# A hybrid attention layer on one core: all K steps of the up blocks at one alignment in SBUF

## The chip, the cores and the metric

The kernel runs on one core of a Trainium2 chip. A core has TensorE (PE: matmuls, and PEld for its weight loads), VectorE (DVE), ScalarE (ACT), GpSimd (POOL) and SyncE (SP, which here issues DMAs). The metric is the device time of one execution in microseconds; the kernel before takes 1034.46 us (median of three runs, 1034.37 to 1036.26).

## The reference

One decoder layer over 16 meta tokens and 256 tokens of width 2048. Only the last part matters for the change, after attention, pooling and the first layer norm:

```python
mix = jnp.concatenate([attn_out, pool_out], axis=-1) @ w_o[l]
h = layer_norm(ALPHA * h + mix, ln1_g[l], ln1_b[l])
# conv_gated_ffn:
z = h @ w_up                                   # 2048 -> 2 x 5632
z = sum(zp[:, j:j + T] * conv_w[j] for j in range(3)) + conv_b
a, g = jnp.split(z, 2, axis=-1)
f = (jax.nn.gelu(a) * g) @ w_down
h = layer_norm(ALPHA * h + f, ln2_g[l], ln2_b[l])
```

All inputs are float32.

## The kernel before

**Precision in two parts.** Every operand of a large product is split into an upper part (rounded to the type that TensorE reads in one pass) and a lower part (the remainder). A product is then three matmuls: upper times upper, lower weights times upper activations, upper weights times lower activations.

**Weight tiles.** The weights come as a stream of tiles of 128 x 2048 float32 (1 MB each): query and value projections, pool columns, 16 blocks of `w_o` (the *output blocks*), then 88 blocks of `w_up` mixed with blocks of `w_down`. SyncE fetches each into `wraw` (three buffers). `split_part` (L166) writes the upper part with ScalarE (L170) and the lower with VectorE (L171) into `whl` (three buffers of 4224 elements), in two halves of 1024 columns. Tiles are asked for two ahead (`weights`, L237).

**A block.** An output or up block is 128 output channels. `product` (L268) goes through its 16 K steps of 128 inputs each. A K step is three matmuls with the weights `whl` stationary and the activations moving, 258 columns wide: first L275 (upper, upper), then twice L278 (for these blocks, which are "turned": lower weights with upper activations, then upper weights with lower activations). Each matmul loads its own 128 x 128 weights, which PEld does while the matmul ahead of it runs. The permutations `K_O` and `K_UP` set in which order the K steps come.

**Places.** Where in `whl` the two parts lie is a setting of the kind of block, in elements: `OUTPUT = (0, 2048, True)` puts the upper part at 0 and the lower at 2048. `UP = (12, 12 + 2112, True, 512, 52)` puts the upper at 12 and the lower at 2124, and has a *lead*: columns from 512 on, that is K steps 4 to 15, lie 52 elements further, at 64 and 2176 plus their column. In bytes modulo 256, the first four K steps (the lead) lie at 12 x 4 = 48, and the other twelve at 64 x 4 = 256, so 0, as the output blocks do. The half of a tile that holds the boundary at 512 is written as two runs of 512 elements with the gap between them (the class `Split` and the helper `like` see to that); the other half is one run of 1024.

**The feed-forward stage.** `plan` puts up blocks and down tiles in turn. The first eight up blocks are *folded* (L956): they run on `fold`, 260 columns wide, before the layer norm's statistics are known. The other 80 run on the normalised `hp`, 258 columns. From the tenth of these on, up to the last, a down tile (`seven`, L862: 9 or 12 matmuls of 512 columns at L873 to L875, `whl` moving this time) follows nearly every up block. Convolution, gate and the sums of the Winograd-like down product follow on ScalarE, VectorE and GpSimd.

Of the kernel before, what the change touches and what calls it, by code (L numbers as in the profile page):

```python
# [98 lines left out]
QUERY = (10, 10 + 2048, False)  # L99
HEAD = (12, 12 + 2048, True)  # L100
OUTPUT = (0, 2048, True)
UP = (12, 12 + 2112, True, 512, 52)
DOWN = (56, 56 + 2048)


def places(n, kind):

    if kind:
        return UP if kind == "up" else DOWN
    return (QUERY, HEAD, OUTPUT)[(n >= 8) + (n >= 26)]  # L110
# [1062 lines left out]
```

## Time and profile before

| | |
|---|---|
| median of three runs | 1034.46 us |
| profiled execution | 1035.45 us, of it the span 1033.7 |
| TensorE busy | 1025.6 us |
| VectorE busy | 890.8 us |
| ScalarE busy | 621.1 us |
| GpSimd busy | 185.4 us |
| mean granted clock of TensorE | 0.998 |
| output blocks | from about 208 to 299 us |
| folded blocks | from about 300 to 347 us |
| up blocks on `hp` | from 347.5 us on, with down tiles from about 400 us on |

A row of the timeline has the start in us, the time in us, the engine, line, operation, what it writes and reads, and how many such instructions were merged. A matmul's own time (278 to 290 ns) is longer than the distance to the next one (115 to 127 ns), since matmuls are pipelined: what a matmul costs is the distance from its start to the next start. A row of the stretch table has the stretch, its length, then busy time and instructions of PE, PEld, DVE, ACT and POOL, the granted clock, the DMA share and GB/s. A row about one line of the kernel has the shortest, median and longest duration in ns and the first and last start.

### The profile page before, as it was taken

To read this page: it belongs to the slowest core of one execution; us is meant where nothing else is said; L and a number is where in the kernel's file an instruction comes from. 1 tells how busy PE (TensorE), PEld (TensorE's weight loads), DVE (VectorE), ACT (ScalarE), POOL (GpSimd) and SP (SyncE) were. 2 spreads that over 40 slices of the span, in tenths; PEclk is the share of its full clock that TensorE was granted. 3 is DMA by queue.
4 is the path that set the end of the run, shared out by engine and by line. 5 is a ranking of instruction groups with operands and counts; after the bars stand their busy time and mean duration, and the time that the engine had idled before them with its cause. 6 is when DMAs were issued, how large, how long until landed. Compare 5 with 4: busy or idle time off the path is not lost.

```text
span 1033.7 us, 19199 instructions
## 1 busy us (share of the span) xinstructions
PE 1025.6 (99%) x7644; PEld 976.8 (94%) x7644; DVE 890.8 (86%) x1401; ACT 621.1 (60%) x1000; POOL 185.4 (18%) x245
## 2 busy tenths in 40 slices
PE   9999999999999999999999999999999999999997
PEld 8999999999999999999999999999999999999986
DVE  6878668758879998998999999989999999999876
ACT  6656346645549855565666556565556565566675
POOL 1200014125430021120121101211112111120031
PEclk9999999999999999999999999999999999999999
DMA  9655643454554578978887788887978779887874
GB/s 328 243 187 210 226 154 106 145 194 168 200 196 137 194 225 242 287 281 288 291 277 266 277 296 275 269 277 266 300 264 286 270 278 288 277 276 274 289 235 142
DMA packets 59754, 250.28 MB, mean 242 GB/s; under 512 B 21734, under 2 KB 22416, under 8 KB 32656
## 3 DMA queue, kind: packets, MB, share of 16 engines
q1 hardware_dynamic: 34592, 230.42, 62.1%
q0 software_dynamic: 7888, 16.14, 8.2%
q10 hardware_dynamic: 17184, 2.49, 1.5%
q8 instruction: 60, 0.98, 0.4%
q14 instruction: 30, 0.25, 0.1%
HBM read 232.50 MB, written 2.11 MB: 227 GB/s over the span
## 4 chain that ended last, share of the span: by engine, by line
PE 94%; issue 2%; DVE 1%; DMA 1%; POOL 1%; ACT 0%; POOLq 0%; SPq 0%; DVEq 0%; ACTq 0%
PE mm L278 47%; PE mm L275 24%; PE at L873 6%; PE at L875 6%; PE at L874 6%; PE mm L349 2%; DMA wraw<-in_w_down 1%; DVE whl L171 1%; PE mm L577 0%; PE at L438 0%; PE at L612 0%; PE at L439 0%; POOL gb L992 0%; DMA wraw<-in_w_first 0%; PE at L324 0%
## 5 line engine op out<-in xcount | busy, mean ns | idle before, releaser
L171 DVE TENSOR_TENSOR whl<-wraw,whl 128x1024 fp32r<-128x1024 f32 (+1 forms) x416 | 486.5, 1204 | 37.0 <-ACT whl L170 36.0
L170 ACT ACTIVATE whl<-wraw 128x1024 fp32r<-128x1024 f32 (+1 forms) x416 | 402.7, 1015 | 99.3 <-DVE wraw L182 20.6
L278 PE MATMUL mm<-hp,whl 128*128 128x258 f32 x2560 | 459.6, 281 | 0.0
L278 PEld LDWEIGHTS mm<-hp,whl 128*128 128x128 f32 x2560 | 395.5, 189 | 3.1
L275 PE MATMUL mm<-hp,whl 128*128 128x258 f32 x1280 | 362.2, 283 | 0.0
L275 PEld LDWEIGHTS mm<-hp,whl 128*128 128x128 f32 x1280 | 240.4, 188 | 3.2
L278 PE MATMUL mm<-xp,whl 128*128 128x256 f32 (+5 forms) x768 | 140.2, 282 | 0.0
L278 PEld LDWEIGHTS mm<-xp,whl 128*128 128x128 f32 x768 | 118.7, 189 | 0.5
L275 PE MATMUL mm<-xp,whl 128*128 128x256 f32 (+5 forms) x384 | 112.0, 292 | 0.0
L808 ACT ACTIVATE z<-mm,cv 128x256 f32<-128x256 f32 x40 | 22.6, 564 | 97.7 <-PE mm L278 97.7
L845 POOL TENSOR_TENSOR forms<-za 128x128 f32<-128x128 f32 x20 | 21.2, 1062 | 307.1 <-DVE za L826 240.5
L275 PEld LDWEIGHTS mm<-xp,whl 128*128 128x128 f32 x384 | 72.2, 188 | 1.0 <-issue 0.5
L875 PE MATMUL at<-whl,gp 128*128 128x512 f32 x180 | 70.7, 394 | 0.0
L874 PE MATMUL at<-whl,gp 128*128 128x512 f32 x180 | 70.7, 394 | 0.0
L873 PE MATMUL at<-whl,gp 128*128 128x512 f32 x180 | 69.4, 395 | 0.0
L808 ACT ACTIVATE za<-mm,cv 128x256 f32<-128x256 f32 x40 | 22.6, 564 | 75.6 <-PE mm L278 67.9
L848 POOL TENSOR_TENSOR forms<-za 128x128 f32<-128x128 f32 x20 | 20.3, 1014 | 199.8 <-DVE za L826 199.8
L278 PE MATMUL mm<-fold,whl 128*128 128x260 f32 x256 | 46.3, 283 | 0.0
L278 PE MATMUL mm<-mixp,whl 128*128 128x258 f32 x256 | 45.4, 278 | 0.0
L278 PE MATMUL mm<-mixa,whl 128*128 128x258 f32 x256 | 45.2, 278 | 0.0
L875 PEld LDWEIGHTS at<-whl,gp 128*128 128x128 f32 x180 | 33.8, 188 | 8.1
L874 PEld LDWEIGHTS at<-whl,gp 128*128 128x128 f32 x180 | 33.9, 188 | 6.8
(339 smaller groups left out, 1607.8 us busy)
## 6 DMA issues: line engine op xcount, KB each, us to landing
wraw<-in_w_up SPq DMA_DIRECT2D x88, 1024.0 KB, 5.0
wraw<-in_w_down SPq DMA_DIRECT2D x80, 1024.0 KB, 6.3
wraw<-in_w_proj SPq DMA_DIRECT2D x24, 1024.0 KB, 5.4
wraw<-in_w_o SPq DMA_DIRECT2D x16, 1024.0 KB, 4.9
y<-v POOLq DMA_DIRECT2D x27, 256.0 KB, 8.5
y<-u POOLq DMA_DIRECT2D x18, 256.0 KB, 4.9
wraw<-in_w_first SPq DMA_DIRECT2D x8, 304.0 KB, 5.4
x<-in_xt SPq DMA_DIRECT2D x1, 2176.0 KB, 8.0
```

The source lines that it names most:

```text
L170: upper = nc.scalar.activation(hl[:, 0, c], like(raw[:, c], hl, c), AF.Copy)
L171: lower = nc.vector.tensor_tensor(hl[:, 1, c], like(raw[:, c], hl, c), hl[:, 0, c].bitcast(F32), op=ALU.subtract)
L275: nc.tensor.matmul(ps, wh, ah, start=n == 0, stop=False)
L278: nc.tensor.matmul(ps, a, b, start=False, stop=i == 1 and n == KT - 1)
L349: nc.tensor.matmul(ps[:m, :T], hl[:, t // 2, a0 + a:a0 + a + m], x_parts[k][:, t % 2, :], start=k == 0 and t == 0, stop=k == KT - 1 and t ...
L808: nc.scalar.activation(z, src[:, 2:NQ], AF.Identity, bias=col(C_B, j), scale=col(C_W, 3 * j + 2))
L845: nc.gpsimd.tensor_tensor(s[:, 0], a21, a22, op=ALU.add)
L848: nc.gpsimd.tensor_tensor(s[:, 3], a11, a21, op=ALU.subtract)
L873: nc.tensor.matmul(ps, a[:, 0, i], hl[:, 0, w], start=j == 0, stop=False)
L874: nc.tensor.matmul(ps, a[:, 0, i], hl[:, 1, w], start=False, stop=False)
L875: nc.tensor.matmul(ps, a[:, 1, i], hl[:, 0, w], start=False, stop=j == n - 1)
```

## The change

The places of the up and folded blocks become those of the output blocks, without a lead:

```diff
 QUERY = (10, 10 + 2048, False)
 HEAD = (12, 12 + 2048, True)
 OUTPUT = (0, 2048, True)
-UP = (12, 12 + 2112, True, 512, 52)
+UP = (0, 2048, True)
 DOWN = (56, 56 + 2048)
```

All sixteen K steps of these 88 blocks then lie at 0 modulo 256 bytes from the start of `whl`, upper and lower; for K steps 4 to 15 that residue is what it was. TensorE's instructions and their order stay the same; only the addresses of the weights differ. On ScalarE and VectorE the half with the boundary becomes one run of 1024. On VectorE among the last output blocks, where the first folded tiles are split (the second row is the first half of such a tile):

```order
 L732 TENSOR_TENSOR x<-x,acc 128x258
-L171 TENSOR_TENSOR whl<-wraw,whl 128x2x512
+L171 TENSOR_TENSOR whl<-wraw,whl 128x1024
 L746 SCALAR_TENSOR_TENSOR fold<-x,cv,fold 128x258
 L171 TENSOR_TENSOR whl<-wraw,whl 128x1024
 L715 SCALAR_TENSOR_TENSOR x<-x,mm 128x258
```

Nothing moved: the shape of the write is all that differs.

## The prediction

> **What bounds the kernel now.** The page comes first, then the stretch table of the feed-forward stage, then TensorE's timeline row by row at the starts of K steps.
>
> ```profile
> span 1033.7 us, 19199 instructions
> PE 1025.6 (99%) x7644; PEld 976.8 (94%) x7644; DVE 890.8 (86%) x1401; ACT 621.1 (60%) x1000; POOL 185.4 (18%) x245
> ...
> PE 94%; issue 2%; DVE 1%; DMA 1%; POOL 1%; ACT 0%; POOLq 0%; SPq 0%; DVEq 0%; ACTq 0%
> ...
> L278 PE MATMUL mm<-hp,whl 128*128 128x258 f32 x2560 | 459.6, 281 | 0.0
> ...
> L275 PE MATMUL mm<-hp,whl 128*128 128x258 f32 x1280 | 362.2, 283 | 0.0
> ```
>
> The chain that ended last is TensorE's for 94% of the span. The two groups are the up blocks on `hp`: 1280 K steps of three matmuls, so 80 blocks of 16 steps. Their busy times overlap (matmuls are pipelined), so I read the cost of a step from start to start. The stretch of the feed-forward stage shows that nothing else holds them up:
>
> ```profile
> 434.00:970.00 536.00, 536.00 (x3854) 505.32 (x3853) 494.41 (x680) 319.16 (x445) 84.52 (x100) 1.00 0.83 279
> ```
>
> TensorE is busy for all 536.00 us at a granted clock of 1.00; VectorE for 494.41 us (92%). The edit must therefore act through the spacing of matmuls that never wait for another engine. That spacing isn't one number. First an output block of 16 steps (its first, its last, and the next block's first row), then two up blocks in a row, with the down matmuls between them:
>
> ```profile
> 266.24 0.28 PE L275 MATMUL mm<-mixp,whl 128*128 128x258 f32 x1
> 271.44 0.28 PE L275 MATMUL mm<-mixp,whl 128*128 128x258 f32 x1
> 271.78 0.28 PE L275 MATMUL mm<-mixp,whl 128*128 128x258 f32 x1
> ...
> 442.51 0.28 PE L275 MATMUL mm<-hp,whl 128*128 128x258 f32 x1
> 443.95 0.28 PE L275 MATMUL mm<-hp,whl 128*128 128x258 f32 x1
> 444.30 0.28 PE L275 MATMUL mm<-hp,whl 128*128 128x258 f32 x1
> 448.11 0.39 PE L873 MATMUL at<-whl,right 128*128 128x512 f32 x1
> ...
> 450.20 0.28 PE L275 MATMUL mm<-hp,whl 128*128 128x258 f32 x1
> 451.63 0.28 PE L275 MATMUL mm<-hp,whl 128*128 128x258 f32 x1
> 451.98 0.29 PE L275 MATMUL mm<-hp,whl 128*128 128x258 f32 x1
> 456.02 0.40 PE L873 MATMUL at<-whl,right 128*128 128x512 f32 x1
> 458.12 0.28 PE L275 MATMUL mm<-hp,whl 128*128 128x258 f32 x1
> ```
>
> The output block takes 271.78 - 266.24 = 5.54 us, 0.346 a step. The first up block spends 1.44 us on its four lead steps (0.36 each) and then (448.11 - 444.30)/11 = 0.346 on each of its last eleven. The second spends 1.43 us on its lead (0.358) and (456.02 - 451.98)/11 = 0.367 on each of the last eleven. So the rest of a block, whose places are already those of the output blocks modulo 256 bytes, runs in one of two steady patterns, **fast** (0.346) and **slow** (0.367), and keeps it to its end. Blocks take 5.60 and 5.82 us in turn; far later it is the same:
>
> ```profile
> 948.61 0.28 PE L275 MATMUL mm<-hp,whl 128*128 128x258 f32 x1
> 954.21 0.39 PE L873 MATMUL at<-whl,right 128*128 128x512 f32 x1
> 956.30 0.28 PE L275 MATMUL mm<-hp,whl 128*128 128x258 f32 x1
> 962.12 0.40 PE L873 MATMUL at<-whl,right 128*128 128x512 f32 x1
> ```
>
> Again 5.60 and 5.82. In the nine blocks ahead of the first down matmuls the order is slow, fast, and a third, **middle** pattern:
>
> ```profile
> 347.54 0.28 PE L275 MATMUL mm<-hp,whl 128*128 128x258 f32 x1
> 353.36 0.29 PE L275 MATMUL mm<-hp,whl 128*128 128x258 f32 x1
> 358.95 0.28 PE L275 MATMUL mm<-hp,whl 128*128 128x258 f32 x1
> 360.72 0.28 PE L275 MATMUL mm<-hp,whl 128*128 128x258 f32 x1
> 364.61 0.29 PE L275 MATMUL mm<-hp,whl 128*128 128x258 f32 x1
> ```
>
> 5.82, 5.59, then 5.66 with (364.61 - 360.72)/11 = 0.354 a step. Equal places, three spacings: the pattern is chosen by the state in which the block is entered, and the lead sits exactly where that choice is made.
>
> **The change part by part.** *Splits.* The first half of each up and folded block is written by ScalarE and VectorE in one run of 1024 elements in place of two of 512. While the folded blocks run, both kinds of halves fall into these two rows:
>
> ```profile
> L171 DVE TENSOR_TENSOR whl<-wraw,whl x14: 1212/1218/1226, 300.9 to 342.6; 128x1024 fp32r<-128x1024 f32 x14
> L170 ACT ACTIVATE whl<-wraw x15: 1036/1048/1062, 299.8 to 343.4; 128x1024 fp32r<-128x1024 f32 x15
> ```
>
> Shortest to longest differ by 14 and 26 ns. The gap costs at most that, over 88 halves 1.2 us on VectorE and 2.3 on ScalarE, under the 8% that VectorE is idle and far more on ScalarE. On the path: nothing; uncovered, at most those sums. If TensorE gains 12 us of some 570, VectorE's share goes from 92 to 94%, still under TensorE's. No DMA, wait or instruction moves.
>
> *Folded blocks*, 260 columns wide:
>
> ```profile
> 318.68 0.28 PE L275 MATMUL mm<-fold,whl 128*128 128x260 f32 x1
> 320.12 0.28 PE L275 MATMUL mm<-fold,whl 128*128 128x260 f32 x1
> 324.45 0.28 PE L275 MATMUL mm<-fold,whl 128*128 128x260 f32 x1
> ```
>
> Lead 1.44/4 = 0.360, the rest 4.33/12 = 0.361: no pattern is held and the lead costs what the rest costs. I take zero; bounds from the fast and slow steps above, 8 x 16 x (0.346 - 0.361) = -1.9 us and +0.8.
>
> *Up blocks.* Sixteen equal steps in a held pattern take 16 x 0.346 = 5.54 us (fast; the output block is the row for it), 16 x 0.354 = 5.66 (middle), 16 x 0.367 = 5.87 (slow). Today a pair takes 5.60 + 5.82 = 11.42. After the nine early blocks 71 remain, 35.5 pairs. All fast: 11.08 a pair, -0.34 x 35.5 = -12.1; the early three cost 364.61 - 347.54 = 17.07 and would cost 16.62, three times -0.45 = -1.4. Together -13.5. All slow: +0.32 x 35.5 + 3 x 0.54 = +13.0. These are the bounds of the one unknown, the pattern.
>
> Which value? The places that the change gives were entered from outside four times in the output stage, the nearest rows:
>
> ```profile
> 208.78 0.28 PE L275 MATMUL mm<-mixp,whl 128*128 128x258 f32 x1
> 209.12 0.28 PE L275 MATMUL mm<-mixp,whl 128*128 128x258 f32 x1
> ...
> 211.67 0.28 PE L275 MATMUL mm<-mixa,whl 128*128 128x258 f32 x1
> 212.73 0.28 PE L275 MATMUL mm<-mixa,whl 128*128 128x258 f32 x1
> ...
> 217.60 0.28 PE L275 MATMUL mm<-mixp,whl 128*128 128x258 f32 x1
> 220.38 0.28 PE L275 MATMUL mm<-mixa,whl 128*128 128x258 f32 x1
> ...
> 239.19 0.28 PE L275 MATMUL mm<-mixp,whl 128*128 128x258 f32 x1
> 240.24 0.28 PE L275 MATMUL mm<-mixp,whl 128*128 128x258 f32 x1
> ```
>
> Steps of 0.34 after the pool blocks, 1.06/3 = 0.353 after the value products, 2.78/8 = 0.348 after the pooled maps, 1.05/3 = 0.35 (0.346 within the rows' rounding) after the mean: three fast, one middle, none slow. And fast held on: the block from 266.24 us, quoted above, comes several blocks after the last of these entries. I take fast for most blocks, with an estimated entry cost of 0.015 us a block (the steps around 239 us are 0.004 over 0.346, taken for four steps: 71 x 0.015 = +1.1) and, also an estimate, one block in six in the middle pattern as the four entries leave room for it (12 x 0.12 = +1.4). Sum: -13.5 + 1.1 + 1.4 = -11.0. The profiled execution took 1035.45 us (1033.7 of span, 1.75 around it), 1.0 over the median of 1034.46; so 1024.4 against the profile, 1023.5 against the median, which is what I predict.
>
> The row that bears on a rule: equal steps of three 128x258 matmuls take 0.346 or 0.367 us. The Trainium skill ("TensorE: Matmul & The Clock Gate", Step-by-step: what each phase is for) says that TensorE reads its moving operand and its weights through two independent ports, so that loading the next weights takes nothing from the running matmul. By that, places could change nothing and the time would stay at 1034.5. The trace shows that equal instructions at full clock do differ by 6%, though not that the ports are why.
>
> **The rivals.**
> *Slow lock.* The run of down matmuls hands every block a state that leads to the slow pattern, and no lead is left to shift it. For it: 35 of 71 blocks now run slow with these very places after step 4, and the state after a slow block recurs. Against: no slow step in the output stage. Price +13.0 in full, 1047.5; it decides from the point where more than half of the blocks are slow (three in four: about +6, 1040.5).
> *Middle pattern for all.* 5.66 a block: -0.10 x 35.5 - 3 x 0.09 = -3.8, so 1030.7. Seen in one of four entries and one of three early blocks.
> *Nothing changes.* Fast and slow blocks still alternate, because the down matmuls flip the state from block to block: 5.54 + 5.87 = 11.41 against 11.42, the lead was worth nothing, 1034.5. The alternation over 560 us speaks for it; that the lead starts alike in both kinds (1.44 and 1.43) and yet parts them speaks against.
>
> **How the numbers follow.** Mostly fast 0.41, middle 0.12, nothing 0.13, slow lock 0.34, in part or in full. Below 1021.5 is less than all fast without any entry cost; above 1043 lies the full slow lock, about 0.17. So the range is 1021.5 to 1043; the likeliest case's own is 1021.5 to 1029. Faster by over 0.2% (what a measurement of this kernel can tell): 0.41 + 0.12 = 0.53; within 0.2%: 0.13; slower: 0.34.
>
> **What would show it.** In TensorE's timeline the first rows (L275) of steps 0 to 15 of every up block stand 0.346 us apart, in the blocks of both turns, and blocks are 5.54 to 5.57 long; folded blocks keep 0.36; the split rows keep 1218 and 1048 ns; VectorE's share rises. Wrong would be steps of 0.367 from the first on, or blocks that still come in two lengths.

## The result, and the profile after

The changed kernel takes 1025.62 us in the median of five runs (1024.8 to 1029.97), the kernel before 1034.48 us beside it: a ratio of 0.9919, 95% interval 0.9896 to 0.9943. The forecast was 1023.5 us, in a range of 1021.5 to 1043. The profiled execution after took 1025.62 us, 9.83 less than that of before (1035.45).

The page of the changed kernel, its lines for the span, the engines, the chain that ended last, the two split groups and the two groups of the up blocks:

```profile
span 1023.8 us, 19199 instructions
...
PE 1016.8 (99%) x7644; PEld 966.6 (94%) x7644; DVE 889.9 (87%) x1401; ACT 622.1 (61%) x1000; POOL 186.7 (18%) x245
...
PE 94%; issue 2%; DMA 1%; DVE 1%; POOL 1%; ACT 0%; SPq 0%; POOLq 0%; DVEq 0%; ACTq 0%
...
L171 DVE TENSOR_TENSOR whl<-wraw,whl 128x1024 fp32r<-128x1024 f32 (+1 forms) x416 | 486.2, 1203 | 43.7 <-ACT whl L170 42.7
L170 ACT ACTIVATE whl<-wraw 128x1024 fp32r<-128x1024 f32 (+1 forms) x416 | 402.5, 1014 | 114.6 <-DMA wraw<-in_w_up 27.9
L278 PE MATMUL mm<-hp,whl 128*128 128x258 f32 x2560 | 450.3, 279 | 0.0
...
L275 PE MATMUL mm<-hp,whl 128*128 128x258 f32 x1280 | 357.6, 279 | 0.0
```

The limit is where it was: TensorE is still 99% busy and 94% of the chain. The up blocks' busy time fell from 459.6 to 450.3 us on L278 and from 362.2 to 357.6 on L275. The stretch of the feed-forward stage (its length; busy us of TensorE, its weight loads, VectorE, ScalarE and GpSimd; then granted clock, DMA share, GB/s):

```profile
434.00:970.00 536.00, 536.00 (x3913) 504.35 (x3912) 499.64 (x687) 325.27 (x452) 85.02 (x100) 1.00 0.85 284
```

TensorE is full here as before, at the same granted clock of 1.00, but does 3913 matmuls in these 536 us where it did 3854. VectorE went from 494.41 to 499.64 us. The time thus came from the spacing of the same matmuls. TensorE's timeline shows it: the first row of block 52 (counted from the query blocks; the first up block on `hp`), then the first row of blocks 54, 61, 66, 68 and 130 with the row behind the block. L275 opens a K step, L873 opens the down matmuls behind the block.

```profile
346.68 0.28 PE L275 MATMUL mm<-hp,whl 128*128 128x258 f32 x1
...
358.02 0.28 PE L275 MATMUL mm<-hp,whl 128*128 128x258 f32 x1
...
363.57 0.28 PE L275 MATMUL mm<-hp,whl 128*128 128x258 f32 x1
...
399.64 0.28 PE L275 MATMUL mm<-hp,whl 128*128 128x258 f32 x1
...
405.51 0.40 PE L873 MATMUL at<-whl,gp 128*128 128x512 f32 x1
...
441.50 0.28 PE L275 MATMUL mm<-hp,whl 128*128 128x258 f32 x1
...
447.36 0.40 PE L873 MATMUL at<-whl,right 128*128 128x512 f32 x1
...
457.12 0.28 PE L275 MATMUL mm<-hp,whl 128*128 128x258 f32 x1
...
462.70 0.40 PE L873 MATMUL at<-whl,gp 128*128 128x512 f32 x1
...
954.86 0.28 PE L275 MATMUL mm<-hp,whl 128*128 128x258 f32 x1
...
960.42 0.39 PE L873 MATMUL at<-whl,right 128*128 128x512 f32 x1
```

Block 54 takes 5.55 us (16 steps of 0.3467), blocks 61 and 66 take 5.87 and 5.86 (the slow pattern), block 68 5.58 and block 130 5.56. Read from the starts of all 1280 steps, blocks 61 to 66 are slow (5.85 on average) and all 65 blocks from 67 to 131 are fast, at 5.569 us each: their first three steps take 0.360, 0.352 and 0.348 us, the others 0.347. Before, 35 of the 71 blocks from 61 on were slow. The 80 up blocks together went from 456.32 to 447.29 us, 9.03 less. A further 0.86 us lies ahead of them (block 52 began at 347.54 us before, and now at 346.68), where the change does almost nothing. It is not the change's work: block 28, ahead of everything that was changed, already began 1.30 us earlier (at 206.43 in place of 207.73), and the 14 profiles of this case have it anywhere from 206.1 to 207.7 us. Together that is the 9.9 us between the two spans.

### The profile page after: what moved, and what is told of

The parts are those of the page before. It is cut to its first block, busy times and chain, and to the rows that moved or that the text cites. A ratio compares the mean times of both kernels' runs of the same rounds, so it can differ in the third digit from the quotient of the medians.

```text
span 1023.8 us, 19199 instructions
## 1 busy us (share of the span) xinstructions
PE 1016.8 (99%) x7644; PEld 966.6 (94%) x7644; DVE 889.9 (87%) x1401; ACT 622.1 (61%) x1000; POOL 186.7 (18%) x245
## 4 chain that ended last, share of the span: by engine, by line
PE 94%; issue 2%; DMA 1%; DVE 1%; POOL 1%; ACT 0%; SPq 0%; POOLq 0%; DVEq 0%; ACTq 0%
PE mm L278 47%; PE mm L275 24%; PE at L875 6%; PE at L873 6%; PE at L874 6%; PE mm L349 1%; DMA wraw<-in_w_down 1%; DVE whl L171 1%; DMA wraw<-in_w_first 1%; POOL gb L992 0%; PE mm L577 0%; PE at L438 0%; PE at L612 0%; PE at L439 0%; PE at L324 0%
## 5 line engine op out<-in xcount | busy, mean ns | idle before, releaser
L171 DVE TENSOR_TENSOR whl<-wraw,whl 128x1024 fp32r<-128x1024 f32 (+1 forms) x416 | 486.2, 1203 | 43.7 <-ACT whl L170 42.7
L170 ACT ACTIVATE whl<-wraw 128x1024 fp32r<-128x1024 f32 (+1 forms) x416 | 402.5, 1014 | 114.6 <-DMA wraw<-in_w_up 27.9
L278 PE MATMUL mm<-hp,whl 128*128 128x258 f32 x2560 | 450.3, 279 | 0.0
L278 PEld LDWEIGHTS mm<-hp,whl 128*128 128x128 f32 x2560 | 390.6, 188 | 3.4
L275 PE MATMUL mm<-hp,whl 128*128 128x258 f32 x1280 | 357.6, 279 | 0.0
L275 PEld LDWEIGHTS mm<-hp,whl 128*128 128x128 f32 x1280 | 240.4, 188 | 3.1
L278 PE MATMUL mm<-xp,whl 128*128 128x256 f32 (+5 forms) x768 | 140.2, 282 | 0.0
L278 PEld LDWEIGHTS mm<-xp,whl 128*128 128x128 f32 x768 | 118.7, 189 | 0.5
L275 PE MATMUL mm<-xp,whl 128*128 128x256 f32 (+5 forms) x384 | 112.0, 292 | 0.0
L275 PEld LDWEIGHTS mm<-xp,whl 128*128 128x128 f32 x384 | 72.3, 188 | 1.0 <-issue 0.5
L875 PE MATMUL at<-whl,gp 128*128 128x512 f32 x180 | 71.2, 396 | 0.0
L874 PE MATMUL at<-whl,gp 128*128 128x512 f32 x180 | 70.6, 393 | 0.0
L873 PE MATMUL at<-whl,gp 128*128 128x512 f32 x180 | 69.5, 396 | 0.0
L278 PE MATMUL mm<-fold,whl 128*128 128x260 f32 x256 | 46.3, 283 | 0.0
L278 PE MATMUL mm<-mixp,whl 128*128 128x258 f32 x256 | 45.6, 279 | 0.0
L278 PE MATMUL mm<-mixa,whl 128*128 128x258 f32 x256 | 45.4, 279 | 0.0
L875 PEld LDWEIGHTS at<-whl,gp 128*128 128x128 f32 x180 | 33.8, 188 | 8.2
L874 PEld LDWEIGHTS at<-whl,gp 128*128 128x128 f32 x180 | 33.8, 188 | 6.8
```

The lines of the kernel that those rows point to most:

```text
L170: upper = nc.scalar.activation(hl[:, 0, c], like(raw[:, c], hl, c), AF.Copy)
L171: lower = nc.vector.tensor_tensor(hl[:, 1, c], like(raw[:, c], hl, c), hl[:, 0, c].bitcast(F32), op=ALU.subtract)
L275: nc.tensor.matmul(ps, wh, ah, start=n == 0, stop=False)
L278: nc.tensor.matmul(ps, a, b, start=False, stop=i == 1 and n == KT - 1)
L873: nc.tensor.matmul(ps, a[:, 0, i], hl[:, 0, w], start=j == 0, stop=False)
L874: nc.tensor.matmul(ps, a[:, 0, i], hl[:, 1, w], start=False, stop=False)
```

## The experiments

All are edits of the changed kernel. Times are compared with the kernel before on the same chip, since its own median differed between chips (1034.5 to 1038.8); block lengths and totals of the 80 up blocks come from the profiles, where the changed kernel has 447.3 us and the kernel before 456.3.

**Is it the equality modulo 256 bytes, or the form?** First the two runs that keep the equality and change something else.

```diff
-UP = (0, 2048, True)
+UP = (0, 2112, True, 512, 64)      # lead and gap kept, the gap 256 bytes
```

> The lead and its gap are kept, but the gap is 64 elements (256 bytes), so all sixteen places are equal modulo 256 bytes and each first half is still written in two runs of 512. Theory of equal places modulo 256 bytes: as the changed kernel, 1025 to 1030, up blocks of 5.57 us. Rival, that the split's form (two runs of 512) cost the time: up blocks of 5.60 and 5.82 us in turn, 1034.5.

Measured 1026.98 us, ratio 0.9924 (0.9909 to 0.9940). The up blocks take 447.3 us in all, as with the change. Block 69:

```profile
464.78 0.28 PE L275 MATMUL mm<-hp,whl 128*128 128x258 f32 x1
...
470.36 0.40 PE L873 MATMUL at<-whl,gp 128*128 128x512 f32 x1
```

5.58 us, the first six blocks behind a down run slow again and the others fast. The split in two runs of 512 costs the path nothing; the places alone make the gain.

```diff
-UP = (0, 2048, True)
+UP = (64, 64 + 2112, True)         # where steps 4 to 15 lay before
```

> The up and folded blocks lie at offset 64 and 64 + 2112 of their tile, which is where steps 4 to 15 lay before the change; there is no lead. Modulo 256 bytes this equals the changed kernel. Theory of the held pattern (equal places modulo 256 bytes hand the pattern on): about the changed kernel's time, 1024.5 to 1030, with equal steps of 0.347 us in most up blocks. Rival, that the lower offsets or the shorter distance between the two halves (2048 in place of 2112 elements) made the gain: 1031 to 1047, with steps of 0.367 us in half of the blocks or more.

Measured 1026.17 us, ratio 0.9921 (0.9890 to 0.9952), 448.1 us of up blocks. From block 61 on every block has the length it has with the change; blocks 53 to 60 ran in the middle pattern (5.65 us) in this execution. Moving all places by 256 bytes changes nothing from there on, as the forecast assumed when it counted places modulo 256 bytes.

**Was the mixture bad, or the lead's places?**

```diff
-UP = (0, 2048, True)
+UP = (12, 12 + 2112, True)         # all sixteen steps at the old lead's places
```

> All sixteen steps of the up and folded blocks lie at the old lead's offset, 12 elements, with the old distance of 2112 between the halves. Theory that only equality counts (any equal place holds some pattern, and mostly the fast one): 1024 to 1030, steps of 0.347 us. Theory that the place counts too, because the weights then stand 32 bytes from the moving operand's places in place of 8: steps of about 0.354 to 0.361 us, as in the old lead and in the folded blocks, and 1280 x (0.354 to 0.361 - 0.349) = 6 to 15 us more than the changed kernel, 1032 to 1041. Rival that the lead's places were bad in themselves and the mixture did nothing: 0.367 us in every step, 1047.

Measured 1036.10 us, ratio 1.0003 (0.9986 to 1.0019). Blocks 69 and 73:

```profile
466.35 0.28 PE L275 MATMUL mm<-hp,whl 128*128 128x258 f32 x1
...
472.12 0.40 PE L873 MATMUL at<-whl,gp 128*128 128x512 f32 x1
...
499.89 0.28 PE L275 MATMUL mm<-hp,whl 128*128 128x258 f32 x1
...
505.54 0.40 PE L873 MATMUL at<-whl,right 128*128 128x512 f32 x1
```

5.77 and 5.65 us: neither the slow pattern nor the fast one, but steps of 0.360 us in block 69 and of 0.353 in block 73. Equality is not enough. Blocks come in groups of four, and the groups follow the down runs: 5.76 us behind a run of twelve down matmuls, 5.65 behind a run of nine. In total 457.5 us, so the mixture of before cost as much as its lead's places used throughout.

```diff
-UP = (0, 2048, True)
+UP = (0, 2112, True, 512, 16)      # lead, then a gap of 64 bytes
```

> The lead of four steps is kept, and each first half is written in two runs of 512 again, but the gap behind the lead is 16 elements (64 bytes) in place of 52 (208 bytes): the lead and the rest are then equal modulo 64 bytes, and differ modulo 256. If equality modulo 64 bytes is enough: 1024.5 to 1030, up blocks of 5.55 to 5.57 us, and the two-run form of the split costs nothing. If it takes equality modulo 256 bytes: blocks in two lengths again, the steps after the lead partly at 0.367 us, 1031 to 1040. If the two-run form of the split was what the time hung on: 1034.5.

Measured 1041.90 us, ratio 1.0071 (1.0048 to 1.0093): slower than before.

```diff
-UP = (0, 2048, True)
+UP = (16, 16 + 2048, True)         # nothing mixed, all 64 bytes later
```

> All sixteen steps of the up and folded blocks lie 16 elements (64 bytes) later than in the changed kernel, at 16 and 16 + 2048; nothing is mixed and nothing else changes. Theory A (only mixing places disturbs; any equal places modulo 64 bytes run alike): 1025 to 1030, steps of 0.347 us. Theory B (the place modulo 256 bytes sets which patterns are there, since the steps behind the gap of 64 bytes ran at 0.361 us in the earlier run): steps of 0.361 us in the up blocks, 1280 x (0.361 - 0.349) = 15 us more, 1037 to 1044, and the folded blocks at 0.353 in place of 0.361, 1 us less.

Measured 1040.70 us, ratio 1.0067 (1.0044 to 1.0091). Rows of the run with everything 64 bytes later: an output block (from its first step to the next block's), a folded block likewise, up block 69, and the group of L278 on its page.

```profile
226.74 0.29 PE L275 MATMUL mm<-mixp,whl 128*128 128x258 f32 x1
...
232.60 0.29 PE L275 MATMUL mm<-mixp,whl 128*128 128x258 f32 x1
...
316.57 0.28 PE L275 MATMUL mm<-fold,whl 128*128 128x260 f32 x1
...
322.22 0.28 PE L275 MATMUL mm<-fold,whl 128*128 128x260 f32 x1
...
471.75 0.28 PE L275 MATMUL mm<-hp,whl 128*128 128x258 f32 x1
...
477.52 0.40 PE L873 MATMUL at<-whl,gp 128*128 128x512 f32 x1
```

```profile
L278 PE MATMUL mm<-hp,whl 128*128 128x258 f32 x2560 | 465.4, 282 | 0.3 <-DVE hp L794 0.3
```

The up block takes 5.77 us, 0.361 a step, as nearly all up blocks do: theory B, the place modulo 256 bytes sets which patterns there are, and equality modulo 64 does not help. The gap of 64 bytes was slow for that reason (its steps behind the gap took 0.361 too, its first three the slow 0.367), so that run says nothing of its own on mixing. The folded block, with 260 columns on `fold`, went the other way, from 5.78 to 5.65 us. That brought nothing: the first up block waits for the last parts of `hp` (the 0.3 us behind VectorE's L794 in the last row, and 0.2 behind ScalarE's), and from folded block 45 to up block 53 it is 46.36 us, against 46.21 with the change. And the output block, whose places no run touched, took 5.86 us in this execution where the profiles of before and after show 5.55 and 5.65.

```diff
-UP = (0, 2048, True)
+UP = (12, 12 + 2112, True)
-        a = Parts(ring.tile([P, 2, WIDE], F32R, tag="act", name="hp"), 2, NQ)
+        a = Parts(ring.tile([P, 2, WIDE], F32R, tag="act", name="hp"), 14, NQ)
```

> The up blocks' weights lie at the old lead's places (12 and 12 + 2112) as in the run with all steps there, and the moving operand hp lies 12 elements later as well, so that weights and moving operand stand to each other as in the changed kernel. Theory of relative places (what counts is how far the weights' bytes are from the moving operand's, modulo 256): the fast pattern is back, 0.347 us a step, 1025 to 1030. Theory of the weights' own place: 0.360 and 0.353 us a step as with the lead's places alone, 1034 to 1037.

Measured 1036.04 us, ratio 1.0012 (1.0003 to 1.0022). Block 69:

```profile
466.35 0.28 PE L275 MATMUL mm<-hp,whl 128*128 128x258 f32 x1
...
472.06 0.40 PE L873 MATMUL at<-whl,gp 128*128 128x512 f32 x1
```

5.71 us: neither the fast pattern (so the distance between weights and moving operand isn't all) nor the steps of 0.360 of the lead's places alone (so `hp`'s place counts as well). Steps of 0.352 and 0.362 us alternate, behind runs of twelve and of nine alike. Both theories fall; both operands' places count, and no rule for the pair came out of it.

**The folded blocks.**

```diff
+LEAD = (12, 12 + 2112, True, 512, 52)
-        return UP if kind == "up" else DOWN
+        return (LEAD if n < 42 + 2 * FOLDED else UP) if kind == "up" else DOWN
```

> The changed kernel with the old lead of four steps given back to the eight folded blocks alone. The forecast's term for the folded blocks was zero: the time stays within 0.7 us of the changed kernel's (1025 to 1030 with its own spread), the folded blocks at 5.78 us each and the first up block entered in another state. Rival, that part of the gain came through the folded blocks: up to 1.9 us more than the changed kernel.

Measured 1026.61 us, ratio 0.9919 (0.9903 to 0.9936), the change's own ratio; folded blocks take 5.77 us. The term of zero holds. The profile also held an accident that no edit could have placed better. In block 109 a pair of matmuls came late, with no wait recorded (0.51 us on the second row, 0.40 in other steps). The rows are the start of 109, that pair, 110's start and end, and 113's start and end.

```profile
788.37 0.28 PE L275 MATMUL mm<-hp,whl 128*128 128x258 f32 x1
788.50 0.51 PE L278 MATMUL mm<-hp,whl 128*128 128x258 f32 x2
...
797.13 0.28 PE L275 MATMUL mm<-hp,whl 128*128 128x258 f32 x1
...
802.99 0.40 PE L873 MATMUL at<-whl,gp 128*128 128x512 f32 x1
...
822.42 0.29 PE L275 MATMUL mm<-hp,whl 128*128 128x258 f32 x1
...
827.98 0.39 PE L873 MATMUL at<-whl,right 128*128 128x512 f32 x1
```

Block 108 was fast (5.57 us). After the late pair 109 was slow, and so were 110 (5.86), 111 and 112, each reached through a run of twelve; 113, the first reached through a run of nine, was fast again (5.56).

**Is the pattern carried?** The same made on purpose, with one overwritten matmul more at five places:

```diff
+EXTRA = {14: 32, 20: 64, 26: 128, 32: 192, 38: 258}
+            n = EXTRA.get(f, 0) * (1 - half_)
+            n and nc.tensor.matmul(ps[:, :n], hl[:, 0, 0:P], h_parts[K_UP[0]][:, 0, :n], start=True, stop=True)
             product(ps[:, :NQ], hl, h_parts, 0, NQ, K_UP, ...)
```

> The changed kernel with one more matmul, whose result the next one overwrites, ahead of the first half's block of five up rows spread over the stage (blocks 72, 84, 96, 108 and 120 counted from the query blocks); it reads the same weights and moving operand and is 32, 64, 128, 192 and 258 columns wide. Work added: at most 5 x 0.12 = 0.6 us. Theory of the held pattern, chosen by the state in which a block is entered: at one or more of the five places the steps change between 0.347 and 0.367 us (or 0.353) and keep the new value through the next blocks and down runs until the next of these places; a flip to slow costs 12 x 0.28 = 3.4 us per stretch, so 1025 to 1043. Rival, that the pattern follows from the places and the instructions alone, and the six slow blocks from the first down runs' form: the block with the extra matmul may differ, the next ones are back at 0.347 us, and the time is 1025.6 + 0.6, at most 1028.

Measured 1028.97 us, ratio 0.9946 (0.9924 to 0.9969). The extra matmul of 192 columns (L971), the end of its block 108, then the starts and ends of 109 and 113:

```profile
779.54 0.25 PE L971 MATMUL mm<-hp,whl 128*128 128x192 f32 x1
...
785.50 0.40 PE L873 MATMUL at<-whl,gp 128*128 128x512 f32 x1
...
788.30 0.28 PE L275 MATMUL mm<-hp,whl 128*128 128x258 f32 x1
...
794.16 0.40 PE L873 MATMUL at<-whl,gp 128*128 128x512 f32 x1
...
822.25 0.29 PE L275 MATMUL mm<-hp,whl 128*128 128x258 f32 x1
...
827.81 0.39 PE L873 MATMUL at<-whl,right 128*128 128x512 f32 x1
```

Blocks 108 to 112 are slow (5.86 us each) and 113 is fast, as in the accident. The 32 columns ahead of block 72 gave middle steps and the 128 ahead of 96 slow ones, each for that one block, because the next came through a run of nine; 64 and 258 columns left the fast pattern. Each theory is half right. A run of twelve down matmuls hands slow on as slow and fast on as fast; a regular run of nine hands on fast from all three patterns. *Regular* means that L873, L874 and L875 come in turn, three matmuls after three; the runs ahead of blocks 61 to 66 are in other orders (the nine ahead of 66 begin with three of L873), and the later ones are all regular. That also explains the flip of the changed kernel: block 67 is the first behind a regular run of nine.

```diff
+EXTRA = {17: 64, 19: 128, 21: 32}
+            n = EXTRA.get(2 * f + half_, 0)
```

(and the extra matmul of the run before)

> The changed kernel with one more matmul, overwritten by the next one, ahead of blocks 61 (64 columns), 63 (128) and 65 (32), three of the six blocks that ran slow in every profile with these places. Work added: about 0.09 to 0.12 us each. Theory of the carried pattern: if one of the three parts the steps from slow, the blocks behind it are fast (or middle) too as far as the run of twelve down matmuls carries the pattern: up to five blocks x 0.28 = 1.4 us less and 0.3 us more, so 1024.5 on the changed kernel's 1025.6. Theory that the first down runs' order of matmuls gives slow whatever comes in: the three blocks change at most in themselves, the others stay at 5.85 us, 1025.9.

Measured 1030.58 us, ratio 0.9926 (0.9903 to 0.9950); not to be told from the change's 0.9919. The extra matmul ahead of block 63, the block's first row, and the first rows of two later steps:

```profile
420.81 0.22 PE L971 MATMUL mm<-hp,whl 128*128 128x128 f32 x1
420.87 0.34 PE L275 MATMUL mm<-hp,whl 128*128 128x258 f32 x1
...
426.05 0.28 PE L275 MATMUL mm<-hp,whl 128*128 128x258 f32 x1
426.40 0.28 PE L275 MATMUL mm<-hp,whl 128*128 128x258 f32 x1
```

Block 63 turned fast (0.35 from the third row to the fourth), and 65 behind the next extra matmul, but 64 was slow again at 5.85 us, and 61 stayed slow. The first down runs, whose matmuls come in another order than later (ahead of blocks 62 to 65 the up block's first matmul stands among them), thus made 64 slow even from a fast block; block 66, slow in all other profiles with these places for up and down weights, was fast behind the fast 65. The up blocks came to 446.6 us, 0.7 less than with the change: too little to show.

**Whose places decide, the up blocks' or the down run's?** Only the down blocks' offset was changed.

```diff
-DOWN = (56, 56 + 2048)
+DOWN = (0, 2048)
```

> The changed kernel with the down blocks' weights at offset 0 in place of 56. They are the moving operand of the down matmuls, 744 in all, which stand 0.233 us apart at 512 columns, some 0.02 us more than 258 columns at the fast step (0.1156 us each) would give per column (0.229). [...] Theory that only the 258-column steps, with a new pair of places every 0.12 us, feel it: 0.233 us as before, and the time moves only by what state the run hands to the next up block, 1025 to 1043.

Measured 1043.47 us, ratio 1.0038 (1.0019 to 1.0056), up blocks 458.7 us. Blocks 69 (behind twelve) and 73 (behind nine):

```profile
465.10 0.28 PE L275 MATMUL mm<-hp,whl 128*128 128x258 f32 x1
...
470.95 0.40 PE L873 MATMUL at<-whl,gp 128*128 128x512 f32 x1
...
499.01 0.28 PE L275 MATMUL mm<-hp,whl 128*128 128x258 f32 x1
...
504.67 0.39 PE L873 MATMUL at<-whl,right 128*128 128x512 f32 x1
```

5.85 us, slow, and 5.66, middle, to the end of the stage. The down matmuls themselves keep their time: from a run's first matmul to the up block behind it, it is 0.2337 us for each in a run of twelve and 0.2327 in a run of nine, against 0.2329 and 0.2333 with the change, and 176.3 us over all of them (756 in the trace; 744 were expected) against 176.2. The up blocks lost 11.4 us with not one of their own bytes moved.

```diff
-DOWN = (56, 56 + 2048)
+DOWN = (40, 40 + 2048)
```

> As the run with the down weights at 0, but at 40 elements, which is 64 bytes below the present place, so that it stays equal modulo 64 bytes and differs modulo 256. [...] Theory that modulo 64 bytes counts: 0.233 us as now, up blocks as now, 1025 to 1030. A different hand-over to the up blocks shows as slow steps of 0.367 us in all of them, up to 1043.

Measured 1034.88 us, ratio 0.9967 (0.9948 to 0.9987), up blocks 455.1 us. Block 69:

```profile
468.00 0.28 PE L275 MATMUL mm<-hp,whl 128*128 128x258 f32 x1
...
473.66 0.39 PE L873 MATMUL at<-whl,gp 128*128 128x512 f32 x1
```

5.66 us: the middle pattern, behind runs of twelve and nine alike, from block 67 to the end. The down matmuls take 175.5 us in all.

```diff
-DOWN = (56, 56 + 2048)
+DOWN = (24, 24 + 2048)
```

> The changed kernel with the down weights at offset 24, the one class of 64 bytes modulo 256 that differs from the places tried so far (56: fast up blocks behind regular runs; 40: the middle step in all; 0: slow behind twelve matmuls and middle behind nine) and is equal to 56 and 40 modulo 64 bytes. Theory that the run of down matmuls hands over the state and its place decides which: the spacing of the down matmuls stays 0.233 us and the up blocks settle at one length for runs of twelve and one for runs of nine, of 5.55 to 5.57, 5.65 or 5.85 us; if fast with no cost at the entry, and from block 61 on, up to 3 us less than the changed kernel; if middle 5 to 6 us more, if slow 18 us more. Theory that the up blocks' own places decide: 5.57 us as with 56, 1025 to 1030.

Measured 1030.74 us, ratio 0.9957 (0.9943 to 0.9970), up blocks 453.0 us. Blocks 73 and 74, both behind runs of nine:

```profile
499.61 0.28 PE L275 MATMUL mm<-hp,whl 128*128 128x258 f32 x1
...
505.45 0.40 PE L873 MATMUL at<-whl,right 128*128 128x512 f32 x1
...
507.56 0.28 PE L275 MATMUL mm<-hp,whl 128*128 128x258 f32 x1
...
513.13 0.39 PE L873 MATMUL at<-whl,right 128*128 128x512 f32 x1
```

5.84 and 5.57 us in turn, though the blocks are equal in all their places: behind runs of nine slow and fast alternate, and behind regular runs of twelve all blocks are fast. Nor is it the block's number that decides: among the first of them the even blocks 66 and 68 are slow (5.84 us) and 67 is fast (5.57), later the odd ones are slow. So a run of nine here turns fast into slow and slow into fast. None of the twelve runs is faster than the changed kernel by more than can be measured.

## Why the prediction was right, and where it was not

**The bound** was right: TensorE stays full, and the edit acts through the spacing of matmuls that wait for nothing.

**Splits at nothing**: right. The split rows of 1024 took 1221 ns (L171) and 1045 (L170) in the median while the folded blocks ran, where it had been 1218 and 1048, and two runs of 512 in place of one of 1024 left the gain whole. **Folded blocks at nothing**: right, 40.4 us for seven of them before and 40.5 after, and the change keeps its ratio with the old lead in them.

**The bound of all-fast blocks, -13.5**: mis-sized. A fast block takes 16 x 0.3467 = 5.547 us, not 5.54, and 80 of them 443.8; against 456.3 that is -12.5. The rounding of a step to 0.346 and the assumption that blocks 61 to 66 alternated too made the difference.

**The entry cost, +1.1**: the right kind, too small. With first steps of 0.360, 0.352 and 0.348 us a block stood 5.569 - 5.547 = 0.022 us over the fast one, in 65 blocks some 1.5 us; 0.015 had been estimated.

**One block in six in the middle pattern, +1.4**: this step named the wrong pattern. No block behind a down run was middle; six were slow, 6 x 0.30 = +1.8, and blocks 52 and 53 cost 0.2. So 12.5 - 1.5 - 1.8 - 0.2 = 9.0 us came from the up blocks, against 11.0 forecast. The 0.9 us ahead of them gave part of that back, which was luck.

**Why fast** was the weakest step. It was argued from four entries of the output stage. What decided was the state that the down runs hand over, and those had been seen only together with the lead. The rivals were not wrong ideas: each is what the same up blocks do behind down weights at another offset. Middle for all is offset 40, with 5.66 us. Alternation without a lead is offset 24 behind runs of nine. Slow is offset 0 behind runs of twelve, and the six blocks 61 to 66 here. So the chances given to them, about one in three for the slow lock and one in eight each for the middle pattern and no change, stood for something real; that the offset of 56 gives fast behind both lengths of run could not be read from the profile of before. That the likeliest case came true was in that part luck.

**That the lead sits exactly where the choice is made** is half of it. All places equal at 12, at 16, or at 12 with `hp` moved along give no fast block behind the runs of twelve and nine. Which patterns exist depends on the places modulo 256 bytes; which of them a block gets depends on the run ahead of it. What the lead alone did at the entry was not separated from these two.

The Trainium skill ("TensorE: Matmul & The Clock Gate", Step-by-step: what each phase is for) says that TensorE reads its moving operand and its weights through two independent ports. The prediction drew from it that places cost nothing, which would have given 1034.5 us. The runs go against that consequence: 64 bytes later, the same instructions take 1040.7 us in place of 1025.6. Whether ports are the reason no run here shows.

## What to carry to other kernels

Where TensorE is full and equal matmuls still come at two spacings, look at starts step by step before looking at other engines: here 6% of a step hung on the operands' places modulo 256 bytes and on what ran just before. Treat the offsets of all weights that follow each other as one table, the neighbours' too, and measure each combination on the chip; a gain found with one neighbour (here the down weights at 56) is lost with another. A faster step ahead of a wait for another engine, as in the folded blocks, brings nothing.

## What the runs showed that was not expected

*A late pair lasts.* One pair of matmuls 0.11 us late cost four slow blocks, 4 x 0.30 = 1.2 us, until a run of nine ended it.

*Stages with no such end keep what they begin with.* The output blocks lie at the same places in every kernel here, and ran at 5.55 us in most profiles, partly at 5.65 in two of them (the changed kernel's is one), and at 5.866 in those with the gap of 64 bytes, with all places 64 bytes later, and with the extra matmuls from block 61. For the first two of these three the profiled executions took 1046.37 and 1045.48 us, where the medians of their kernels are 1041.90 and 1040.70. The 14 blocks from 30 to 43 at 0.32 us more are 4.5 us, about that difference. Blocks 53 to 60 vary in the same way (5.55, 5.65 or 5.87). On the chip that ran the extra matmuls from block 61 and the down weights at 0 and 40, the kernel before shows two groups: three of its 20 executions took 1034.6 to 1035.7 us, the other 17 took 1038.3 to 1040.7. The run with the down weights at 0 has its profile at 1037.07 us, with output blocks at 5.55, and its median at 1043.47. There the totals of the up blocks say more than the medians. That the spread of the changed kernel's runs, 1024.8 to 1029.97 us, comes from there as well is likely by its size, and so it is for these two kernels, but it was not shown run by run.

*Open* stays why bytes modulo 256 matter, why nine down matmuls end a slow pattern that twelve pass on, and whether some pair of offsets for up and down weights gives fast blocks without the entry cost and from block 61 on. Nor was it tested whether the order slow, fast, middle of blocks 52 to 60 in the kernel before follows the three buffers of `whl`. With the changed kernel's places they don't decide: the same blocks ran in all three patterns, from one execution to another.
